# A chunked scan beside a projection stream: products inside chunks in longer runs, decays prepared on ScalarE, loads and gate units re-ordered

## The chip, the cores and the metric

The kernel runs on one core of a Trainium2 chip. The metric is device time in microseconds, the median of several executions of the whole program; lower is better. TensorE multiplies matrices, VectorE and ScalarE work on elements, GpSimd does little here, and SyncE (SP) issues the DMA transfers, one after another.

## The reference, cut to what matters

One layer of a hybrid backbone on 1152 tokens (1024 latent tokens in eight chunks of 128, and 128 context tokens, chunk 8). The change lies in the Mamba-2 scan, which runs in two directions for 32 heads of 64 channels:

```python
a_cs = cumsum(a within the chunk)                   # a = dt * A
L = exp(where(mask, a_cs[i] - a_cs[j], -inf))
CB = einsum("bcign,bcjgn->bcgij", Cc, Bc)
y_diag = einsum("bcgrij,bcjgrp->bcigrp", CB[:, :, :, None] * L, x)      # inside chunks
states = einsum("bcjgn,bcgrj,bcjgrp->bcgrpn", Bc, exp(a_cs[..., -1:] - a_cs), x)
h_final, h_prev = scan(h -> exp(a_cs[..., -1]) * h + states)            # from chunk to chunk
y_off = einsum("bcign,bcgri,bcgrpn->bcigrp", Cc, exp(a_cs), h_prev)     # from earlier chunks
y = y_diag + y_off          # then both directions are added, + D * x, times silu(z)
```

Here x carries a factor dt. Around the scan stand an input projection of 1024 by 9280 columns (z, x, B, C, dt, u, v and two branch gates ga, gb), a gated MLP branch, the merge, the output projection and a ConvFFN. All is float32.

## The kernel before

**Stages.** The projection is done in blocks of 128 output channels. One block takes 3 token blocks of 384 and 24 matmuls for each (8 contraction blocks, and a high and a low part of each factor: hi*hi, lo*hi, hi*lo). Its matmuls write the PSUM tile `gps` (lines 301 to 303, three banks). Weights come in tiles of 128x512 (`wr`); ScalarE makes the high part (`wh`, line 84) and VectorE the low part (`wl`, line 85). `conv_gen` (x, B, C), `z_unit` and `gate_unit` use the result; a gate unit only copies it out (line 610) and stores it.

**The scan beside it.** The scan works on 16 pairs of heads, q = 0 to 15, four to a group of B and C. `rounds[q]` lists the projection blocks that run while pair q is scanned: x of the next pair, z of the pair before, at the end of a group also B and C of the next, and `NGATE[q]` gate units. `merge` spreads the scan's steps evenly over the round's block slots (3 to a block). Steps are raised in priority by `P_SCAN` = 50. Each engine's instructions are put in order when the program is built, by priority and planned time, and run on the chip in that order.

**A pair's steps.** With s = 0 to 3 for two chunks each and s = 4 for the context chunk:

- `ssd_loads(q, s)`: SP loads `R` (the cumulative sums of both directions and heads, spread over the partitions, three buffers), `EP` (the same for the factor of `y_off`, two buffers), and with s = 4 the start state `H`.
- `mstage(s)`: makes exp(a_cs - a_cs' + ln dt) from R. The shift by `nb` goes to ScalarE for the first four of up to eight pieces (`NACT`, line 672) and to VectorE for the rest (line 674, with a clamp at 60). VectorE clamps the first four (line 677), ScalarE takes the exponentials of R (line 678) and EP (line 680), VectorE multiplies by `CB` (line 688) and adds the directions (line 689).
- `chain(s)`: the states. VectorE scales Xtok into `xwf`, `xwb` (line 694), TensorE multiplies by B into the one bank `pst` (lines 709, 710), VectorE carries `H` along (lines 713, 715).
- `ctx_state()`: the context's final state through the same bank (line 724), copied out (line 725).
- `main(s)`: TensorE makes `yo` (from the states, line 740) and `yd` (inside chunks, line 744: for each chunk one matmul per head, each on 64 of the 128 columns of the array, `tile_position=(0, 64 * h)`). VectorE joins them with X (lines 749 to 754).

The order of a pair's steps:

```python
pro = [step((mstage, 4), (chain, 0)), step((mstage, 0), (chain, 1)), step((chain, 2)), step((chain, 3))]
outs = [step((mstage, 1), (main, 4), (ssd_loads, q, 2)), step((mstage, 2), (main, 0), (ssd_loads, q, 3), (ctx_state,)),
        step((mstage, 3), (main, 1), (nxt, 4)), step((main, 2), (nxt, 0)), step((main, 3), (nxt, 1))]
```

A round holds the five `outs` of its pair and, unless a new group begins, the four `pro` of the next; the first round of a group also its own `pro`: 13, 9, 9 and 5 steps. In the trace a float32 matmul of the scan is two records, so a `main` of two chunks leaves eight records of line 744.

**Ahead of the scan.** `decays` turns dt into `nb` = ln dt - a_cs (line 513), `wst`, `cdk`, and stores the cumulative sums for the loads.

**Behind it.** The scan's memory is given to the gated MLP's tiles, among them `wsT`, which the matmul of line 849 reads.

Of the kernel before, what the change touches and what calls it, by code (L numbers as in the profile page):

```python
# [4 lines left out]
F32 = mybir.dt.float32  # L5
F32R = mybir.dt.float32r
AF = mybir.ActivationFunctionType
# [7 lines left out]
NL = 1024  # L15
# [15 lines left out]
MT_DT, MT_U, MT_B, MT_C, MT_X, MT_Z, MT_GA, MT_GB = 0, 1, 9, 13, 17, 33, 49, 57  # L31


NGATE = [1, 1, 1, 0, 1, 1, 1, 0, 1, 1, 1, 0, 1, 1, 1, 0, 0]

NACT = 4

NXM, NWM, GBUF = 4, 10, 7

# [1 line left out]

LASTK = 4

P_SCAN, P_HT, P_MOD, P_DECAY = 50, 100, 200, 200


def gcol(t):
    return t if t < NL else t + 1
# [60 lines left out]
def body(tc, A, O):  # L109
# [202 lines left out]
    def tbank(name):  # L312
        return pt_.tile([128, 512], F32, tag="t", name=name)
# [134 lines left out]
    k_cm, kp = pool("tok")  # L448
    nb = kp.tile([128, NC, 64], F32, name="nb")
    wst = kp.tile([128, NC, 64], F32, name="wst")  # L450
    cdk = kp.tile([128, 8, 2, 32], F32, name="cdk")
    sb_cm, spb = pool("ssdB")
    u_cm, up = pool("dt")
# [29 lines left out]
    def decays():  # L483
        for src, dst in ((xd, dtt), (xa, adt)):
            ps = tbank("pdt")
            for i in range(4):
                PE.transpose(ps[:, 128 * i:128 * i + 128], src[:, 128 * i:128 * i + 128], ident)
            pv = ps.rearrange("p (c m) -> p c m", m=128)
            S.copy(dst[:, 0:4, :], pv[:, :, 0:64])
            V.tensor_copy(dst[:, 5:9, :], pv[:, :, 64:128])  # L490
        ps = tbank("pdt4")
        for j, src in enumerate((xd, xa)):
            PE.transpose(ps[:, 128 * j:128 * j + 128], src[:, 512:640], ident)
        for j, dst in enumerate((dtt, adt)):
            V.tensor_copy(dst[:, 4, :], ps[:, 128 * j:128 * j + 64])
        for d in range(2):
            a_d = adt[:, :, 32 * d:32 * d + 32]
            for lhs, dst in (((Lo, Up)[d], acst), (ones, tot)):
                pv = tbank(f"pacs{d}")[:, :288].rearrange("p (c h) -> p c h", h=32)
                PE.matmul(pv, lhsT=lhs, rhs=a_d, start=True, stop=True)  # L500
                V.tensor_copy(dst[:, :, 32 * d:32 * d + 32], pv)
        rows = up.tile([64, NC, 128], F32, name="rows")
        for b in range(3):
            ps = tbank(f"prow{b}")
            for i in range(3):
                PE.transpose(ps[:64, 128 * i:128 * i + 128], acst[:, 3 * b + i, :], ident)
            V.tensor_copy(rows[:, 3 * b:3 * b + 3, :], ps[:64, :384].rearrange("p (c m) -> p c m", m=128))
        for d in range(2):
            for h in range(2):
                SP.dma_start(acs_scr[:, d, h], rows[32 * d + h:32 * d + 32:2, :, :])  # L510
        V.tensor_scalar(lndt, dtt, 1e-18, None, op0=ALU.max)
        S.activation(lndt, lndt, AF.Ln)
        V.tensor_tensor(nb, lndt, acst, op=ALU.subtract)
        V.tensor_tensor(wst, tot, acst, op=ALU.subtract)
        S.activation(wst, wst, AF.Exp)
        V.tensor_tensor(wst, wst, dtt, op=ALU.mult)
        S.activation(cdk[:, :, 0, :], tot[:, 0:8, 0:32], AF.Exp)
        for k in range(8):
            S.activation(cdk[:, k, 1, :], tot[:, 7 - k, 32:64], AF.Exp)
# [107 lines left out]
    def cc_of(s):  # L627
        return [2 * s, 2 * s + 1] if s < 4 else [8]

    Rt, EPt, Ht = {}, {}, {}  # L630

    def ssd_loads(q, s):

        cc = cc_of(s)
        n = len(cc)
        R = spa.p.tile([128, 2, 2, 2, 128], F32, tag="R", name=f"R{q}{s}", bufs=3)
        if n == 2:
            SP.dma_start(R.rearrange("p d h c i -> p (d h) (c i)"),
                         acs_scr[q, :, :, cc[0]:cc[0] + 2].rearrange("d h c i -> (d h) (c i)").unsqueeze(0).to_broadcast([128, 4, 256]))
        else:  # L640
            SP.dma_start(R[:, :, :, 0, :].rearrange("p d h i -> p (d h) i"),
                         acs_scr[q, :, :, cc[0]].rearrange("d h i -> (d h) i").unsqueeze(0).to_broadcast([128, 4, 128]))
        Rt[q, s] = R
        if s < 4:
            E = spa.p.tile([128, 2, 2, 128], F32, tag="EP", name=f"EP{q}{s}", bufs=2)
            for h in range(2):
                SP.dma_start(E[64 * h:64 * h + 64].rearrange("p d c i -> p d (c i)"),
                             acs_scr[q, :, h, cc[0]:cc[0] + 2].rearrange("d c i -> d (c i)").unsqueeze(0).to_broadcast([64, 2, 256]))
            EPt[q, s] = E
        if s == 4:  # L650
            H = spa.p.tile([128, 8, 2, 128], F32, tag="H", name=f"H{q}", bufs=2)
            SP.dma_start(H[:, 0], A["h0"][q])
            Ht[q] = H

    def ssd(q):

# [1 line left out]
        _, Bt, CT, CB = groups[g]  # L658
        X, Xt = xq[q]
        Dc = par[:, P_D + q:P_D + q + 1]  # L660

        def mstage(s):
            cc = cc_of(s)
            n = len(cc)
            R = Rt[q, s]
            for d in range(2):
                for h in range(2):
                    col = 32 * d + 2 * q + h
                    for i, c in enumerate(cc):
                        r = R[:, d, h, i, :]  # L670
                        if 4 * d + 2 * h + i < NACT:
                            S.activation(r, r, AF.Identity, bias=nb[:, c, col:col + 1])  # L672
                        else:
                            V.tensor_scalar(r, r, nb[:, c, col:col + 1], 60.0, op0=ALU.add, op1=ALU.min)
            Rv = R.rearrange("p d h c i -> p (d h) c i")[:, :, :n]
            if NACT:
                V.tensor_scalar(Rv[:, :NACT // 2], Rv[:, :NACT // 2], 60.0, None, op0=ALU.min)
            S.activation(Rv, Rv, AF.Exp)
            if s < 4:
                S.activation(EPt[q, s], EPt[q, s], AF.Exp)  # L680
            for d in range(2):
                if n == 2:
                    r = R[:, d].rearrange("p h c i -> p h (c i)")
# [2 lines left out]
                    r = R[:, d, :, 0, :]  # L686
                    cb = CB[:, d, cc[0], :].unsqueeze(1).to_broadcast([128, 2, 128])
                V.tensor_tensor(r, r, cb, op=ALU.mult)
            V.tensor_tensor(R[:, 0, :, :n], R[:, 0, :, :n], R[:, 1, :, :n], op=ALU.add)

        def xw(c0, n, d, dst):

# [24 lines left out]
        def ctx_state():  # L717
# [7 lines left out]
            S.copy(so, ps[:, 0])  # L725
            for d in range(2):
                SP.dma_start(O[2 + d][0, 0, 2 * q:2 * q + 2].rearrange("h p n -> (h p) n"), so[:, d, :])

        def main(s):
            cc = cc_of(s)  # L730
            n = len(cc)
            R = Rt.pop((q, s))
            o = gcol(128 * cc[0])
            if s < 4:
                H = Ht[q]
                yo = pyo.tile([128, 2, 2, 128], F32, tag="yo", name=f"yo{q}{s}")
                for i, c in enumerate(cc):
                    for d in range(2):
                        k = c if d == 0 else 7 - c
                        PE.matmul(yo[:, d, i, :], lhsT=H[:, k, d, :], rhs=CT[:, 128 * c:128 * c + 128], start=True, stop=True)  # L740
            yd = pyd.tile([128, 512], F32, tag="yd", name=f"yd{q}{s}")[:, :128 * n]
            for i, c in enumerate(cc):
                for h in range(2):
                    PE.matmul(yd[64 * h:64 * h + 64, 128 * i:128 * i + 128], lhsT=Xt[:, c, 64 * h:64 * h + 64],  # L744
                              rhs=R[:, 0, h, i, :], start=True, stop=True, tile_position=(0, 64 * h))
            xv = X[:, o:o + 128 * n]
            if s < 4:
                E = EPt.pop((q, s))
                V.tensor_tensor(E, E, yo, op=ALU.mult)
                V.scalar_tensor_tensor(xv, xv, Dc, E[:, 0].rearrange("p c i -> p (c i)"), op0=ALU.mult, op1=ALU.add)  # L750
                V.tensor_tensor(xv, xv, E[:, 1].rearrange("p c i -> p (c i)"), op=ALU.add)
                V.tensor_tensor(xv, xv, yd, op=ALU.add)
            else:
                V.scalar_tensor_tensor(xv, xv, Dc, yd, op0=ALU.mult, op1=ALU.add)

        def nxt(s):
            if q + 1 < 16:
                ssd_loads(q + 1, s)

        def step(*fs):  # L760
            def run():
                for f, *a in fs:
                    f(*a)
            return run
        pro = [step((mstage, 4), (chain, 0)), step((mstage, 0), (chain, 1)), step((chain, 2)), step((chain, 3))]
        outs = [step((mstage, 1), (main, 4), (ssd_loads, q, 2)), step((mstage, 2), (main, 0), (ssd_loads, q, 3), (ctx_state,)),
                step((mstage, 3), (main, 1), (nxt, 4)), step((main, 2), (nxt, 0)), step((main, 3), (nxt, 1))]
        return pro, outs

    def merge(fills, steps):  # L770
# [35 lines left out]
    gtp.p, gtp.bufs = spa.p, 1  # L806
    run_unit(first_x)
    for s in (4, 0, 1):
        ssd_loads(0, s)
    after = None  # L810
    for q in range(17):
        steps = []
# [538 lines left out]
```

## Time and profile before

| | us |
|---|---|
| median of 3 runs (2471.34 to 2474.54) | 2472.48 |
| the profiled execution | 2474.21 |
| its span, first to last instruction | 2472.1 |
| TensorE (PE) busy | 2428.6 |
| VectorE (DVE) busy | 1853.4 |
| ScalarE (ACT) busy | 1110.5 |

PE is matmuls and PEld weight loads, which overlap them. A row of the timeline gives start, length, engine, line, operation, tiles (out<-in), shapes and how many records of a kind follow each other; matmuls are pipelined, so a record's length is more than the time to the next one's start. A group's row gives the busy time and the mean of one, and behind the second bar the engine's idle time before it and what ended it. In square brackets stands the idle time before a single row.

### The profile page before, as it was taken

The numbers are of one execution on the slowest core, as the hardware profiler recorded it, in microseconds if no ns is written. First come the engines' busy times: TensorE is split into PE (matmuls) and PEld (weight loads), VectorE is DVE, ScalarE is ACT, GpSimd is POOL, SyncE is SP. The second block draws the span as 40 slices with busy tenths as digits, with TensorE's granted clock in tenths as the row PEclk, the third lists the DMA queues.
The fourth block names the chain that finished last, engine by engine and source line by source line (L and its number), as shares of the span: only waits on it lengthen the run. The fifth ranks groups of instructions, "written<-read, shape, count | busy, mean of one in ns | idle before, by whom it ended". The sixth has DMA issues, their size and how long they took to land.

```text
span 2472.1 us, 37398 instructions
## 1 busy us (share of the span) xinstructions
PE 2428.6 (98%) x13951; PEld 2271.1 (92%) x13951; DVE 1853.4 (75%) x3150; ACT 1110.5 (45%) x2118; POOL 28.4 (1%) x82
## 2 busy tenths in 40 slices
PE   7989999999999999999999999999999999999998
PEld 5989999999999998899999998999999999998777
DVE  5668988878878884983546657459999989998554
ACT  5545655555555553211445545354333433344443
POOL 0000000000000000000000000000000000000000
PEclk9999999999999999999999999999999999999999
DMA  6134334433433444641456657442212221114674
GB/s 257 39 96 146 123 125 141 136 95 117 140 101 103 149 123 157 214 150 62 148 163 206 210 161 237 153 139 76 71 65 71 69 68 61 66 64 135 217 244 132
DMA packets 204182, 323.21 MB, mean 131 GB/s; under 512 B 19329, under 2 KB 113313, under 8 KB 203873
## 3 DMA queue, kind: packets, MB, share of 16 engines
q1 hardware_dynamic: 204000, 320.82, 40.5%
q8 instruction: 110, 1.80, 0.3%
q14 instruction: 72, 0.58, 0.1%
HBM read 278.22 MB, written 42.52 MB: 130 GB/s over the span
## 4 chain that ended last, share of the span: by engine, by line
PE 89%; DMA 6%; DVE 2%; ACT 1%; issue 1%; SPq 0%; POOL 0%; DVEq 0%; POOLq 0%; ACTq 0%
PE gps L301 10%; PE gps L303 10%; PE gps L302 10%; PE pup L302 7%; PE pup L303 7%; PE pup L301 7%; PE fo L1167 4%; PE fo L1169 4%; PE fo L1168 4%; PE yo L740 2%; PE yd L744 2%; PE pbs L301 2%; PE pbs L302 2%; PE pbs L303 2%; PE pv L865 1%; PE pv L866 1%
## 5 line engine op out<-in xcount | busy, mean ns | idle before, releaser
L85 DVE TENSOR_TENSOR wl<-wr,wh 128x512 fp32r<-128x512 f32 x544 | 371.7, 689 | 250.5 <-ACT wh L84 241.7
L84 ACT CAST wh<-wr 128x512 fp32r<-128x512 f32 x544 | 333.9, 619 | 471.3 <-PE pup L302 121.6
L301 PE MATMUL gps<-hh,wh 128*128 128x384 f32 x1512 | 518.2, 343 | 0.2 <-ACT pad L356 0.2
L303 PE MATMUL gps<-hh,wl 128*128 128x384 f32 x1512 | 513.9, 340 | 0.0
L302 PE MATMUL gps<-hl,wh 128*128 128x384 f32 x1512 | 513.4, 340 | 0.0
L1155 DVE SCALAR_TENSOR_TENSOR acc<-U,fpar,acc 128x960 f32<-128x960 f32 (+1 forms) x352 | 444.3, 1267 | 16.0 <-ACT acc L1148 8.2
L302 PE MATMUL pup<-h2l,wh 128*128 128x384 f32 x1056 | 353.1, 334 | 0.0
L301 PE MATMUL pup<-h2h,wh 128*128 128x384 f32 x1056 | 352.9, 334 | 0.0
L303 PE MATMUL pup<-h2h,wl 128*128 128x384 f32 x1056 | 352.4, 334 | 0.0
L301 PEld LDWEIGHTS gps<-hh,wh 128*128 128x128 f32 x1512 | 284.8, 188 | 6.4 <-issue 5.5
L302 PEld LDWEIGHTS gps<-hl,wh 128*128 128x128 f32 x1512 | 284.9, 188 | 3.9 <-issue 3.8
L303 PEld LDWEIGHTS gps<-hh,wl 128*128 128x128 f32 x1512 | 284.6, 188 | 4.1 <-issue 4.1
L301 PEld LDWEIGHTS pup<-h2h,wh 128*128 128x128 f32 x1056 | 198.2, 188 | 1.3
L302 PEld LDWEIGHTS pup<-h2l,wh 128*128 128x128 f32 x1056 | 198.2, 188 | 1.3
L303 PEld LDWEIGHTS pup<-h2h,wl 128*128 128x128 f32 x1056 | 198.2, 188 | 0.0
L1137 ACT COPY U<-pup 128x384 f32<-128x384 f32 (+1 forms) x132 | 58.4, 443 | 225.1 <-PE pup L303 225.1
L672 ACT ACTIVATE R<-R,nb 128x128 f32<-128x128 f32 x288 | 93.2, 391 | 136.6 <-DMA R<-acs_scr 132.5
L1167 PE MATMUL fo<-wh,gh 128*128 128x512 f32 x384 | 148.1, 397 | 0.3 <-ACT wh L84 0.3
L1168 PE MATMUL fo<-wh,gl 128*128 128x512 f32 x384 | 148.3, 396 | 0.0
L1169 PE MATMUL fo<-wl,gh 128*128 128x512 f32 x384 | 139.8, 396 | 0.0
L301 PE MATMUL pbs<-ysh,wh 128*128 128x384 f32 x384 | 129.8, 338 | 3.6 <-ACT wh L84 1.8
L303 PE MATMUL pbs<-ysh,wl 128*128 128x384 f32 x384 | 129.7, 338 | 0.2
(303 smaller groups left out, 3965.7 us busy)
## 6 DMA issues: line engine op xcount, KB each, us to landing
wr<-in_w_dn SPq DMA_DIRECT2D x132, 256.0 KB, 2.9
wr<-in_w_in SPq DMA_DIRECT2D x130, 256.0 KB, 2.9
R<-acs_scr SPq DMA_DIRECT2D x64, 512.0 KB, 4.1
wr<-in_w_bs SPq DMA_DIRECT2D x96, 256.0 KB, 3.4
wr<-in_w_up SPq DMA_DIRECT2D x90, 256.0 KB, 2.6
EP<-acs_scr SPq DMA_DIRECT2D x128, 128.0 KB, 3.2
wmt<-in_w_modt SPq DMA_DIRECT2D x32, 512.0 KB, 3.8
wr<-in_w_bu SPq DMA_DIRECT2D x48, 256.0 KB, 2.8
```

The costliest lines, as they stand in the source:

```text
L84: self.nc.scalar.copy(hi, w)
L85: self.nc.vector.tensor_tensor(lo, w, hi.bitcast(F32), op=ALU.subtract)
L301: PE.matmul(ps, lhsT=wh, rhs=xh, start=first and k == 0, stop=False)
L302: PE.matmul(ps, lhsT=wh, rhs=xl, start=False, stop=False)
L303: PE.matmul(ps, lhsT=wl, rhs=xh, start=False, stop=last and k == n - 1)
L672: S.activation(r, r, AF.Identity, bias=nb[:, c, col:col + 1])
L740: PE.matmul(yo[:, d, i, :], lhsT=H[:, k, d, :], rhs=CT[:, 128 * c:128 * c + 128], start=True, stop=True)
L1137: S.copy(u[:, a // 64:b // 64, 1:65], src.rearrange("p (r c) -> p r c", c=64))
L1155: tap = V.scalar_tensor_tensor(av[:, r0:r1], u[:, r0 + dy - 1:r1 + dy - 1, dx:dx + 64], w[i], av[:, r0:r1], op0=ALU.mult, op1=ALU.add)
L1167: PE.matmul(outs[c][h], lhsT=mh[:, cs_], rhs=wh, start=k == 0, stop=False)
L1168: PE.matmul(outs[c][h], lhsT=ml[:, cs_], rhs=wh, start=False, stop=False)
L1169: PE.matmul(outs[c][h], lhsT=mh[:, cs_], rhs=wl, start=False, stop=k == NFF - 1)
```

## The change

- **Runs.** The yd part of `main` becomes `within(b)`: four chunks at once for b = 0 (issued after main(1)), four and the context chunk for b = 1 (after main(3)). The summed R goes to a tile `RS` of four chunks; the context chunk's product goes to the unused half of `ctx_state`'s PSUM bank. The matmuls are raised by `P_RUN` = 400, and each is ordered behind the first of its run. `main` keeps yo.
- **Shift and clamp.** `nb` becomes a_cs - ln dt + top, where `top` is the largest ln dt of all. ScalarE takes relu(nb - R) for all pieces and exp(top - that); both clamps on VectorE go.
- **Order.** `chain` comes ahead of `mstage` in `pro`. Loads are split into `load_R`, `load_E`, `load_H`; E of s = 2, 3 is loaded a step later, and its exponential is taken in `main`.
- **Gate units.** `NGATE` is 2, 1, 0, 0 in each group where it was 1, 1, 1, 0.

```diff
-NGATE = [1, 1, 1, 0, 1, 1, 1, 0, 1, 1, 1, 0, 1, 1, 1, 0, 0]
-NACT = 4
+NGATE = [2, 1, 0, 0, 2, 1, 0, 0, 2, 1, 0, 0, 2, 1, 0, 0, 0]
-P_SCAN, P_HT, P_MOD, P_DECAY = 50, 100, 200, 200
+P_SCAN, P_HT, P_MOD, P_DECAY, P_RUN = 50, 100, 200, 200, 400
 # decays
-        V.tensor_tensor(nb, lndt, acst, op=ALU.subtract)
+        V.tensor_reduce(top, lndt.rearrange("p c m -> p (c m)"), axis=AX.X, op=ALU.max)
+        tops = up.tile([128, 128], F32, name="tops")
+        V.tensor_copy(tops, top.to_broadcast([128, 128]))
+        ps = tbank("ptop")
+        PE.transpose(ps[:, :128], tops, ident)
+        V.tensor_reduce(top, ps[:, :128], axis=AX.X, op=ALU.max)
+        V.tensor_tensor(nb, acst, lndt, op=ALU.subtract)
+        V.tensor_scalar(nb, nb, top, None, op0=ALU.add)
 # mstage
-                        if 4 * d + 2 * h + i < NACT:
-                            S.activation(r, r, AF.Identity, bias=nb[:, c, col:col + 1])
-                        else:
-                            V.tensor_scalar(r, r, nb[:, c, col:col + 1], 60.0, op0=ALU.add, op1=ALU.min)
+                        S.activation(r, r, AF.Relu, scale=-1.0, bias=nb[:, c, col:col + 1])
-            if NACT:
-                V.tensor_scalar(Rv[:, :NACT // 2], Rv[:, :NACT // 2], 60.0, None, op0=ALU.min)
-            S.activation(Rv, Rv, AF.Exp)
+            S.activation(Rv, Rv, AF.Exp, scale=-1.0, bias=top)
...
-            V.tensor_tensor(R[:, 0, :, :n], R[:, 0, :, :n], R[:, 1, :, :n], op=ALU.add)
+            V.tensor_tensor(sum_, R[:, 0, :, :n], R[:, 1, :, :n], op=ALU.add)
 # ctx_state
+            RS[3] = ps[:, 1, 0, :]
...
+        def within(b):
+            yd = pyd.tile([128, 512], F32, tag="yd", name=f"yd{q}{b}")
+            todo = [(yd[:, 128 * i:128 * i + 128], 4 * b + i, RS[b][:, :, i]) for i in (2, 3, 0, 1)]
+            if b == 1:
+                yc = RS[3]
+                todo.append((yc, 8, RS[2][:, :, 0]))
+            first = None
+            with tc.high_priority(offset=P_RUN):
+                for p, c, r in todo:
+                    for h in range(2):
+                        m = PE.matmul(p[64 * h:64 * h + 64], lhsT=Xt[:, c, 64 * h:64 * h + 64], rhs=r[:, h, :],
+                                      start=True, stop=True, tile_position=(0, 64 * h))
+                        if first is None:
+                            first = m
+                        else:
+                            queue_behind(m, first)
+            xv = X[:, 512 * b:512 * b + 512]
+            V.tensor_tensor(xv, xv, yd, op=ALU.add)
+            if b == 1:
+                xv = X[:, gcol(NL):gcol(NL) + 128]
+                V.scalar_tensor_tensor(xv, xv, Dc, yc, op0=ALU.mult, op1=ALU.add)
...
-        pro = [step((mstage, 4), (chain, 0)), step((mstage, 0), (chain, 1)), step((chain, 2)), step((chain, 3))]
+        pro = [step((chain, 0), (mstage, 4)), step((chain, 1), (mstage, 0)), step((chain, 2)), step((chain, 3))]
+        outs = [step((mstage, 1), (load_R, q, 2)), step((mstage, 2), (main, 0), (load_R, q, 3), (load_E, q, 2), (ctx_state,)),
+                step((mstage, 3), (main, 1), (within, 0), (load_E, q, 3), (nxt, load_R, 4), (nxt, load_H)),
+                step((main, 2), (nxt, load_R, 0), (nxt, load_E, 0)), step((main, 3), (within, 1), (nxt, load_R, 1), (nxt, load_E, 1))]
 # before round 0
-        ssd_loads(0, s)
+        load_R(0, s)
+        if s < 4:
+            load_E(0, s)
+    load_H(0)
```

More of the change, by code (lines that the diff above doesn't have):

```diff
@@ L450, in body @@
     wst = kp.tile([128, NC, 64], F32, name="wst")
+    top = kp.tile([128, 1], F32, name="top")
     cdk = kp.tile([128, 8, 2, 32], F32, name="cdk")
@@ L630, in body, with load_R @@
     Rt, EPt, Ht = {}, {}, {}
-    def ssd_loads(q, s):
+    def load_R(q, s):
         cc = cc_of(s)
-        n = len(cc)
         R = spa.p.tile([128, 2, 2, 2, 128], F32, tag="R", name=f"R{q}{s}", bufs=3)
-        if n == 2:
+        if len(cc) == 2:
             SP.dma_start(R.rearrange("p d h c i -> p (d h) (c i)"),
@@ L643, in ssd_loads, with load_E, load_H @@
         Rt[q, s] = R
[L644 to L653, printed above, removed]
+    def load_E(q, s):
+        cc = cc_of(s)
+        E = spa.p.tile([128, 2, 2, 128], F32, tag="EP", name=f"EP{q}{s}", bufs=2)
+        for h in range(2):
+            SP.dma_start(E[64 * h:64 * h + 64].rearrange("p d c i -> p d (c i)"),
+                         acs_scr[q, :, h, cc[0]:cc[0] + 2].rearrange("d c i -> d (c i)").unsqueeze(0).to_broadcast([64, 2, 256]))
+        EPt[q, s] = E
+    def load_H(q):
+        H = spa.p.tile([128, 8, 2, 128], F32, tag="H", name=f"H{q}", bufs=2)
+        SP.dma_start(H[:, 0], A["h0"][q])
+        Ht[q] = H
     def ssd(q):
@@ L660, in ssd @@
         Dc = par[:, P_D + q:P_D + q + 1]
+        RS = {}
         def mstage(s):
@@ L664, in mstage @@
             n = len(cc)
-            R = Rt[q, s]
+            R = Rt.pop((q, s))
+            if s == 4:
+                RS[2] = spa.p.tile([128, 2, 1, 128], F32, tag="RSc", name=f"RSc{q}", bufs=2)
+            elif s % 2 == 0:
+                RS[s // 2] = spa.p.tile([128, 2, 4, 128], F32, tag="RS", name=f"RS{q}{s}", bufs=2)
+            sum_ = RS[s // 2][:, :, 2 * (s % 2):2 * (s % 2) + n]
             for d in range(2):
@@ L670, in mstage @@
                         r = R[:, d, h, i, :]
-                        if 4 * d + 2 * h + i < NACT:
-                            S.activation(r, r, AF.Identity, bias=nb[:, c, col:col + 1])
-                        else:
-                            V.tensor_scalar(r, r, nb[:, c, col:col + 1], 60.0, op0=ALU.add, op1=ALU.min)
+                        S.activation(r, r, AF.Relu, scale=-1.0, bias=nb[:, c, col:col + 1])
             Rv = R.rearrange("p d h c i -> p (d h) c i")[:, :, :n]
-            if NACT:
-                V.tensor_scalar(Rv[:, :NACT // 2], Rv[:, :NACT // 2], 60.0, None, op0=ALU.min)
-            S.activation(Rv, Rv, AF.Exp)
+            S.activation(Rv, Rv, AF.Exp, scale=-1.0, bias=top)
             if s < 4:
-                S.activation(EPt[q, s], EPt[q, s], AF.Exp)
+                exp_E(s)
             for d in range(2):
@@ L688, in mstage, with exp_E @@
                 V.tensor_tensor(r, r, cb, op=ALU.mult)
-            V.tensor_tensor(R[:, 0, :, :n], R[:, 0, :, :n], R[:, 1, :, :n], op=ALU.add)
+            V.tensor_tensor(sum_, R[:, 0, :, :n], R[:, 1, :, :n], op=ALU.add)
+        def exp_E(s):
+            if s < 2:
+                S.activation(EPt[q, s], EPt[q, s], AF.Exp)
         def xw(c0, n, d, dst):
@@ L727, in ctx_state @@
                 SP.dma_start(O[2 + d][0, 0, 2 * q:2 * q + 2].rearrange("h p n -> (h p) n"), so[:, d, :])
+            RS[3] = ps[:, 1, 0, :]
         def main(s):
             cc = cc_of(s)
[L731 to L740, printed above, removed]
@@ L741, in main @@
-            yd = pyd.tile([128, 512], F32, tag="yd", name=f"yd{q}{s}")[:, :128 * n]
-            for i, c in enumerate(cc):
[L743 to L754, printed above, removed]
@@ L756, in nxt @@
-        def nxt(s):
+            o = 128 * cc[0]
+            H = Ht[q]
+            yo = pyo.tile([128, 2, 2, 128], F32, tag="yo", name=f"yo{q}{s}")
+            for i, c in enumerate(cc):
+                for d in range(2):
+                    k = c if d == 0 else 7 - c
+                    PE.matmul(yo[:, d, i, :], lhsT=H[:, k, d, :], rhs=CT[:, 128 * c:128 * c + 128], start=True, stop=True)
+            xv = X[:, o:o + 256]
+            E = EPt.pop((q, s))
+            if s >= 2:
+                S.activation(E, E, AF.Exp)
@@ new lines, in main @@
+            V.tensor_tensor(E, E, yo, op=ALU.mult)
+            V.scalar_tensor_tensor(xv, xv, Dc, E[:, 0].rearrange("p c i -> p (c i)"), op0=ALU.mult, op1=ALU.add)
+            V.tensor_tensor(xv, xv, E[:, 1].rearrange("p c i -> p (c i)"), op=ALU.add)
+        def within(b):
[7 more added lines that the diff above has]
+                for p, c, r in todo:
+                    for h in range(2):
+                        m = PE.matmul(p[64 * h:64 * h + 64], lhsT=Xt[:, c, 64 * h:64 * h + 64], rhs=r[:, h, :],
[9 more added lines that the diff above has]
+                V.scalar_tensor_tensor(xv, xv, Dc, yc, op0=ALU.mult, op1=ALU.add)
@@ L757, in nxt @@
+        def nxt(f, *a):
             if q + 1 < 16:
-                ssd_loads(q + 1, s)
+                f(q + 1, *a)
         def step(*fs):
@@ L764, in step @@
             return run
-        pro = [step((mstage, 4), (chain, 0)), step((mstage, 0), (chain, 1)), step((chain, 2)), step((chain, 3))]
-        outs = [step((mstage, 1), (main, 4), (ssd_loads, q, 2)), step((mstage, 2), (main, 0), (ssd_loads, q, 3), (ctx_state,)),
-                step((mstage, 3), (main, 1), (nxt, 4)), step((main, 2), (nxt, 0)), step((main, 3), (nxt, 1))]
+        pro = [step((chain, 0), (mstage, 4)), step((chain, 1), (mstage, 0)), step((chain, 2)), step((chain, 3))]
+        outs = [step((mstage, 1), (load_R, q, 2)), step((mstage, 2), (main, 0), (load_R, q, 3), (load_E, q, 2), (ctx_state,)),
+                step((mstage, 3), (main, 1), (within, 0), (load_E, q, 3), (nxt, load_R, 4), (nxt, load_H)),
+                step((main, 2), (nxt, load_R, 0), (nxt, load_E, 0)), step((main, 3), (within, 1), (nxt, load_R, 1), (nxt, load_E, 1))]
         return pro, outs
```

## The prediction

> **What bounds the kernel now.** I read the page's shares and chain first, then the busy time by stretches, then TensorE's waits, and last the order of TensorE's instructions inside the scan.
>
> ```profile
> span 2472.1 us, 37398 instructions
> PE 2428.6 (98%) x13951; PEld 2271.1 (92%) x13951; DVE 1853.4 (75%) x3150; ACT 1110.5 (45%) x2118; POOL 28.4 (1%) x82
> PE 89%; DMA 6%; DVE 2%; ACT 1%; issue 1%; SPq 0%; POOL 0%; DVEq 0%; POOLq 0%; ACTq 0%
> ```
> ```profile
> 60.00:145.00 85.00, 77.95 (x448) 74.18 (x446) 56.27 (x91) 44.34 (x85) 0.30 (x3) 0.96 0.21 62
> 145.00:950.00 805.00, 804.20 (x5210) 761.84 (x5210) 663.49 (x1480) 437.94 (x848) 3.96 (x36) 1.00 0.39 121
> 950.00:1216.00 266.00, 262.15 (x1410) 242.20 (x1409) 163.31 (x300) 56.74 (x100) 4.54 (x3) 0.99 0.47 153
> ```
> ```profile
> PE ptX L549 <- ACT Xtok L550: 5.7, 2, 4.9
> PE prs L849 <- DMA wsT<-in_sgu_w: 3.2, 1, 3.2
> PE pst L709 <- DVE xwf L694: 0.2, 1, 0.2
> ```
>
> The columns of the second fence are the stretch, its length, then busy time of PE, PEld, DVE, ACT, POOL, then granted clock and DMA. The scan is the stretch 145 to 950: TensorE is busy for 804.2 of 805 us, VectorE for 663, ScalarE for 438. So time is won there only by taking work from TensorE's queue; VectorE and ScalarE matter where they make it wait, and the third fence says they hardly do: the large wait, 4.9 us, lies ahead of the scan, the next, 3.2 us, behind it.
>
> But busy is not free of loss. The rows below show TensorE around the products inside chunks (yd, line 744).
>
> ```profile
> 947.45 0.33 PE L301 MATMUL gps<-hh,wh 128*128 128x384 f32 x1
> 947.62 0.34 PE L302 MATMUL gps<-hl,wh 128*128 128x384 f32 x1
> 947.89 0.66 PE L744 MATMUL yd<-R,Xtok 128*64 128x128 f32 x8
> 948.48 0.44 PE L303 MATMUL gps<-hh,wl 128*128 128x384 f32 x1
> 948.76 0.34 PE L301 MATMUL gps<-hh,wh 128*128 128x384 f32 x1
> ```
> ```profile
> 249.37 0.34 PE L301 MATMUL gps<-hh,wh 128*128 128x384 f32 x1
> 249.64 0.44 PE L744 MATMUL yd<-R,Xtok 128*64 128x128 f32 x4
> 250.01 0.45 PE L302 MATMUL gps<-hl,wh 128*128 128x384 f32 x1
> 250.29 0.34 PE L303 MATMUL gps<-hh,wl 128*128 128x384 f32 x1
> ```
> ```profile
> 526.15 0.42 PE L302 MATMUL gps<-hl,wh 128*128 128x384 f32 x1
> 526.50 0.43 PE L744 MATMUL yd<-R,Xtok 128*64 128x128 f32 x2
> 526.86 0.44 PE L303 MATMUL gps<-hh,wl 128*128 128x384 f32 x1
> ...
> 528.70 0.43 PE L744 MATMUL yd<-R,Xtok 128*64 128x128 f32 x2
> 529.06 0.45 PE L303 MATMUL gps<-hh,wl 128*128 128x384 f32 x1
> 529.34 0.34 PE L301 MATMUL gps<-hh,wh 128*128 128x384 f32 x1
> ```
>
> Undisturbed, gps matmuls start 0.17 us apart (947.45, 947.62). With eight yd records between, the second gps behind starts 948.76 - 947.62 = 1.14 us after the last one ahead: 1.14 - 2 x 0.17 = 0.80 us for two chunks. With four records: 250.29 - 249.37 - 0.34 = 0.58 us for one chunk. So a visit to yd costs 0.36 us fixed (2 x 0.58 - 0.80) and 0.22 us a chunk. The fixed part sits at its ends: 0.27 us ahead of it and 0.28 us behind its first successor, where 0.17 is normal. In the third fence one main is torn into four visits of two records (one head each): 529.34 - 526.15 = 3.19 us less five spacings (0.85) is 2.34 us, 0.58 us each, where the same work in one visit takes 0.80.
>
> **Part 1: runs of four.** How many visits are there?
>
> ```profile
> L744 PE MATMUL yd<-R,Xtok x576: 272/273/324, 150.7 to 948.3; 128*64 128x128 f32 x192
> 150.68 0.44 PE L744 MATMUL yd<-R,Xtok 128*64 128x128 f32 x4
> ```
>
> The 576 records form, in order of start, 109 stretches without another line between: 53 of eight, 3 of six, 14 of four, 39 of two; the first is this row at 150.68, the last that at 947.89. Cost now: 56 x 0.80 + 14 x 0.58 + 39 x 0.58 = 75.5 us. After: `within(0)` issues four chunks and `within(1)` five, raised by P_RUN and ordered behind their first matmul, so 32 visits: 16 x (0.36 + 0.88) + 16 x (0.36 + 1.10) = 43.2 us. Gain 32.3 us. If visits are torn as often as now, only the merging counts, 3 fewer visits for each of 16 q: 48 x 0.36 = 17.3 us. I take 32.3: each run's first matmul waits for the newest sum (chunks 2 and 3), so the others have nothing left to wait for, and 400 against 50 puts them ahead of the gps stream that tears them now. On VectorE, 64 adds of yd become 32 of double width; it is not the bound.
>
> **Part 2: shift and clamp on ScalarE.**
>
> ```profile
> L672 ACT ACTIVATE R<-R,nb 128x128 f32<-128x128 f32 x278 | 89.9, 391 | 128.1 <-DMA R<-acs_scr 124.0 <-PE gps L303 2.3 <-PE yd L744 1.7
> L674 DVE TENSOR_SCALAR R<-R,nb 128x128 f32<-128x128 f32 x278 | 62.8, 281 | 46.4 <-DMA R<-acs_scr 45.9
> L677 DVE TENSOR_SCALAR R<-R 128x512 f32<-128x512 f32 (+1 forms) x78 | 30.8, 395 | 3.8 <-ACT R L672 3.4
> ```
> ```profile
> 139.56 0.88 DVE L674 TENSOR_SCALAR R<-R,nb 128x128 f32<-128x128 f32 x4 [2.94 <-DMA R<-acs_scr]
> 139.56 1.28 ACT L672 ACTIVATE R<-R,nb 128x128 f32<-128x128 f32 x4 [2.28 <-DMA R<-acs_scr]
> ...
> 144.37 1.06 ACT L678 ACTIVATE R<-R 128x1024 f32<-128x1024 f32 x1
> ```
>
> 288 shifts (16 q x 18; 278 of them inside the scan's stretch) move from line 674 to ScalarE and the 80 clamps of line 677 go. Four in a row take 1.28 us on ScalarE, 0.32 each: +92 us, 438 to 530 in a scan of some 773, 69%. VectorE loses 63 + 31 us and falls to about 570, 74%. Neither is full, so the cost for TensorE is nothing while the slack holds; the rivals price it gone. The Trainium skill, ScalarE: Activation LUTs, rules for kernel authors, sends relu, min and add to VectorE and not to ScalarE. The rows agree on the unit price (0.32 against 0.22 us), and by that rule the move loses 0.10 x 288 = 29 us of engine time; the sum ignores it, since TensorE waits for neither. Relu is not in this trace. If it forced ScalarE to change tables around each of 72 stages, two loads each would cost 72 x 2 x 1.28 = 185 us of ScalarE; at the other end nothing.
>
> ```profile
> L512 ACT ACT_TABLE_LOAD x1 | 1.3, 1283 | 0.0
> ```
>
> I take nothing: identity, exp, tanh and square alternate through the whole scan and it holds no table load. The same page, section on table sets, says relu stands in every set.
>
> The bound `top` adds to the decays a maximum over 576 columns, a broadcast copy, one transpose and its maximum, and a second pass over nb.
>
> ```profile
> 124.60 0.75 DVE L513 TENSOR_TENSOR nb<-lndt,acst 128x576 f32<-128x576 f32 x1
> ```
>
> At this row's 0.75 us or less for each of two wide passes, and less for the narrow ones, that is up to 2.5 us of VectorE in a stretch where TensorE already idles 7 us; hidden it is 0. I take +1.
>
> **Part 3: chain first, loads split.** The 4.9 us wait ahead of the scan is a transpose of X waiting for the Xtok copy, which stands on ScalarE behind R's shifts (139.56, after 2.28 us for R's landing). With eight shifts and the exponential no longer waiting for a clamp, that copy could come 1.28 + 1.06 us later; with the H load behind the R loads and chain, which needs Xtok, first, it could come before them. Bounds -4.9 and +2.4; I take -1, the middle. The SP queue carries the same loads; E of steps 2 and 3 no longer stands with its R, and R's buffer is free after the sum and not after the matmul, so SP blocks less; I count nothing, because TensorE waits for no load in the scan. `yc` now sits in the one pst bank from ctx_state to the end of within(1), so chain(0) of the next q queues behind a VectorE add. The present wait of that matmul is 0.2 us in all; bounds 0 and 15 x 1 us, I take +1.
>
> **Part 4: gate units.** Twelve before, twelve after, 72 gps matmuls each (12.4 us). Rounds 0, 4, 8, 12 gain one, rounds 2, 6, 10, 14 lose one: there 9 steps stand beside 6 block slots, 24.8 us of gps. In round 14 the loss thins what covers the scan's end.
>
> ```profile
> 965.56 2.50 PE L849 MATMUL prs<-wsT,cst 128*128 128x512 f32 x4 [3.20 <-DMA wsT<-in_sgu_w]
> ```
>
> This wait hangs on the scan's memory coming free, after the last yd at 947.89. A later scan end lengthens it: 0 to 12.4 us, I take +2, near the present wait. For new waits inside the scan, 0 to 34 (rival 2), I take +1.
>
> **Sum.** The profiled execution took 2474.2 us (span 2472.1), 1.7 above the median of 2472.5. 2474.2 - 32.3 + 1 - 1 + 1 + 2 + 1 = 2445.9; against the median 2444.
>
> **Rivals.**
> 1. *Half the gain* (chance 0.2): visits are still torn, or starts and tail take the rest: 2472.5 - 17.3, and the other terms' +4: 2459. For it: 39 of 109 visits are torn now. Against: the new order and priority.
> 2. *ScalarE decides the thin rounds* (chance 0.14: 0.04 still faster, 0.05 the same, 0.05 slower).
>
> ```profile
> ACT EP L680 <- DMA EP<-acs_scr: 52.4, 40, 3.9
> ```
>
> Per q ScalarE has 530 / 16 = 33 us of work and (124 + 52) / 16 = 11 us of waiting for R and EP, which hold up all behind them, weight casts and evacuations of gps: 44 us. A thin round gives TensorE 24.8 + about 11 us of scan matmuls. Not absorbed by the next round (12 slots, 49.5 us), that is 8.5 x 4 = 34 us: 2444 + 34 = 2478, slower, and more if landings take longer. From two thirds not absorbed on (23 of 34 us) the gain is gone to within 0.2%; slower needs nearly all of it. Against it: in the whole scan 16 x 44 = 706 us stays under 773, and R's earlier release shortens the waits.
> 3. *The visit's fixed price isn't saved* (0.05): if it belonged to each chunk, the visits of eight would cost 1.16 and not 0.80; then 2472.
>
> **How the numbers follow.** Forecast 0.61, rivals 0.2, 0.14, 0.05. A measurement can tell 0.2%, 5 us: faster means under 2467.5. Faster 0.61 + 0.2 + 0.04 = 0.85; same 0.05 + 0.05 = 0.10; slower 0.05. The range runs from 2433 (the wait ahead of the scan gone too, and no new waits) to 2465 (rival 1 with a thinner tail). The forecast's own range is 2433 to 2453.
>
> **What would show it.** Line 744's successor in 32 visits of 16 and 20 records, some 1.25 and 1.45 us each; TensorE's scan stretch near 773 us and still full; ScalarE near 530, VectorE near 570; no table load. Wrong if visits of two remain, if gps waits for wh or for a bank behind relu, or if prs waits over 10 us.

## The result, and the profile after

The changed kernel takes 2454.97 us (median of 4 runs, 2451.83 to 2456.71) against 2473.51 us of the kernel before in the same sessions: ratio 0.9922, 95% interval 0.9905 to 0.9939, 18.5 us faster. The forecast was 2444 with a range of 2433 to 2465; the direction held, and two thirds of the forecast gain arrived. The profiled execution took 2456.7 us, 17.5 less than that of before.

The page of the changed kernel, with its span, its shares and its chain:

```profile
span 2454.9 us, 37306 instructions
PE 2401.7 (98%) x13952; PEld 2270.2 (92%) x13952; DVE 1782.0 (73%) x2754; ACT 1193.9 (49%) x2406; POOL 27.7 (1%) x82
PE 85%; DMA 6%; DVE 4%; ACT 4%; issue 1%; SPq 1%; POOL 0%; DVEq 0%; ACTq 0%; POOLq 0%
```

The stretches of the scan up to the first v matmul, which starts at 940.06 and started at 956.04 before (columns as in the prediction), first in the kernel before, then in the changed one, here with the stretch behind it:

```profile
145.00:956.00 811.00, 810.20 (x5244) 767.84 (x5244) 666.42 (x1483) 442.04 (x854) 3.96 (x36) 1.00 0.39 121
```
```profile
145.00:940.00 795.00, 781.44 (x5244) 765.47 (x5244) 594.83 (x1092) 522.52 (x1133) 3.54 (x36) 0.99 0.40 123
940.00:1200.00 260.00, 256.90 (x1362) 236.27 (x1363) 160.79 (x297) 52.15 (x94) 4.53 (x3) 0.98 0.47 155
```

TensorE has 28.8 us less to do in the scan (781.4 us, was 810.2), but it is no longer full: it is idle for 13.6 us, where it was idle for 0.8. So the scan is 16 us shorter where 32 less, and TensorE still full, were forecast. VectorE fell from 666 to 595, ScalarE rose from 442 to 523. TensorE's waits say where it stands now:

```profile
PE pv L900 <- ACT vwh L82: 7.6, 1, 7.6
PE yo L755 <- DMA H<-in_h: 4.8, 1, 4.8
PE yd L775 <- DVE X L782: 3.1, 4, 1.3
PE prs L884 <- DMA wsT<-in_sgu_w: 2.8, 1, 2.8
...
PE yo L755 <- DVE H L731: 0.9, 1, 0.9
PE pst L725 <- DVE H L731: 0.7, 2, 0.5
```

The first row is new at this length; in the kernel before that wait was:

```profile
PE pv L865 <- ACT vwh L84: 0.4, 1, 0.4
```

The second row stands where the transposes of X waited 4.9 us. The third row and the last two lie inside the scan, which had almost no waits (0.8 us). TensorE's order around the products, a visit of 16 records and one of 20 (16 into yd, 4 into the context bank):

```profile
387.33 0.34 PE L301 MATMUL gps<-hh,wl 128*128 128x384 f32 x1
387.60 1.09 PE L775 MATMUL yd<-RS,Xtok 128*64 128x128 f32 x16
388.62 0.44 PE L299 MATMUL gps<-hh,wh 128*128 128x384 f32 x1
388.90 0.33 PE L300 MATMUL gps<-hl,wh 128*128 128x384 f32 x1
```
```profile
422.70 0.34 PE L300 MATMUL gps<-hl,wh 128*128 128x384 f32 x1
422.97 1.09 PE L775 MATMUL yd<-RS,Xtok 128*64 128x128 f32 x16
423.89 0.39 PE L775 MATMUL pstc<-RSc,Xtok 128*64 128x128 f32 x4
424.21 0.45 PE L301 MATMUL gps<-hh,wl 128*128 128x384 f32 x1
424.49 0.34 PE L299 MATMUL gps<-hh,wh 128*128 128x384 f32 x1
```

Less two spacings of 0.17 us these are 388.90 - 387.33 - 0.34 = 1.23 us and 424.49 - 422.70 - 0.34 = 1.45 us; 1.24 and 1.46 were forecast. All 32 visits are whole: 16 of each kind, 42.9 us at these two prices where 75.5 were. The Trainium skill, TensorEngine Tiling (Array Packing), key properties, says that a change of the tiling mode drains TensorE; the trace fits it, with a fixed price of 0.36 us a visit.

### The profile page after: what moved, and what is told of

Its sections match the earlier page's. It is cut to its first block, busy times and chain, and to the rows that moved or that the text cites. A ratio compares the mean times of both kernels' runs of the same rounds, so it can differ in the third digit from the quotient of the medians.

```text
span 2454.9 us, 37306 instructions
## 1 busy us (share of the span) xinstructions
PE 2401.7 (98%) x13952; PEld 2270.2 (92%) x13952; DVE 1782.0 (73%) x2754; ACT 1193.9 (49%) x2406; POOL 27.7 (1%) x82
## 4 chain that ended last, share of the span: by engine, by line
PE 85%; DMA 6%; DVE 4%; ACT 4%; issue 1%; SPq 1%; POOL 0%; DVEq 0%; ACTq 0%; POOLq 0%
PE gps L299 9%; PE gps L300 9%; PE gps L301 9%; PE pup L300 7%; PE pup L299 7%; PE pup L301 7%; PE fo L1202 4%; PE fo L1204 4%; PE fo L1203 4%; PE pbs L299 2%; PE pbs L301 2%; PE pbs L300 2%; PE yo L755 2%; DMA R<-acs_scr 1%; PE pv L900 1%
## 5 line engine op out<-in xcount | busy, mean ns | idle before, releaser
L688 ACT ACTIVATE R<-R,nb 128x128 f32<-128x128 f32 x576 | 179.6, 392 | 47.2 <-DMA R<-acs_scr 46.8
```

The source lines that it names most:

```text
L688: S.activation(r, r, AF.Relu, scale=-1.0, bias=nb[:, c, col:col + 1])
```

## The experiments

Ratios are to the kernel before on the same chip, with 95% intervals.

### The runs alone

```diff
 # the kernel before, with RS, within(0), within(1) and P_RUN of the change
-step((mstage, 1), (main, 4), (ssd_loads, q, 2))
+step((mstage, 1), (ssd_loads, q, 2))
-step((mstage, 3), (main, 1), (nxt, 4))
+step((mstage, 3), (main, 1), (within, 0), (nxt, 4))
-step((main, 3), (nxt, 1))
+step((main, 3), (within, 1), (nxt, 1))
```

> The kernel before with the longer runs alone (the tile RS, within(0) and within(1), P_RUN); shift, clamp, order of chain, loads and gate units as before. Theory A (the gain is the visits to the products' array mode, 109 to 32, 32 us of TensorE): TensorE's rows of yd in 32 visits of 16 and 20 records, 1.23 and 1.44 us each, and with the old gate units still covering the scan's end the time is 2442 to 2450. Rival B (VectorE must be relieved of shift and clamp before TensorE can use the gain): VectorE over 90% in the scan, new waits of TensorE on VectorE's sums of over 10 us in all, time 2455 to 2466.

Measured: 2521.65 us, ratio 1.0191 (1.0177 to 1.0206), 47 us slower. The visits were whole, 16 and 16. Both theories miss the time. B names the right engine, but VectorE is not full (636.5 of the 805 us from 145 to 950), and TensorE waits for H and not for the sums. TensorE's longest waits:

```profile
PE pst L715 <- DVE H L721: 38.9, 5, 10.8
```

The pst matmul is chain's. All five waits stand in the third pair of a group (they end at 276.5 and 287.6, 504.7, 727.0 and 933.5); why there, no run shows. Here is the first, VectorE ahead (its own queue in order), then TensorE:

```profile
268.46 0.41 DVE L721 TENSOR_TENSOR H<-H,pst 128x256 f32<-128x256 f32 x1
...
270.26 0.41 DVE L683 TENSOR_SCALAR R<-R 128x512 f32<-128x512 f32 x1
270.60 0.86 DVE L680 TENSOR_SCALAR R<-R,nb 128x128 f32<-128x128 f32 x4
271.38 0.41 DVE L719 TENSOR_TENSOR H<-H,cdk 128x256 f32<-128x256 f32 x1
...
272.65 0.41 DVE L683 TENSOR_SCALAR R<-R 128x512 f32<-128x512 f32 x1
272.99 0.86 DVE L680 TENSOR_SCALAR R<-R,nb 128x128 f32<-128x128 f32 x4
273.77 0.41 DVE L683 TENSOR_SCALAR R<-R 128x512 f32<-128x512 f32 x1
...
275.98 0.41 DVE L721 TENSOR_TENSOR H<-H,pst 128x256 f32<-128x256 f32 x1
```
```profile
276.53 0.77 PE L715 MATMUL pst<-xwf,Btok 128*128 128x128 f32 x2 [6.50 <-DVE H L721]
```

chain(0)'s second add of H (275.98) frees the one pst bank for chain(1). Between chain's instructions on VectorE stand shifts (line 680) and clamps (683), 3 us of the 7.5 from 268.46, beside other work. TensorE stands in front of its matmul with gps behind it. The 38.9 us are not the whole loss. The other waits in the scan add up to 17.8 us, the first v tile waits 8.0 longer than before, and the clock of TensorE stood at half for more of its work (46.5 us, was 15.4; at half the pace an estimated 15.5 us lost, see the last section). With the 32.6 us that the visits save this gives some +48; the profiled executions differ by 46.6.

### Which of the two: the held bank or VectorE's queue

```diff
 # the runs alone, and
-                todo.append((yc, 8, RS[2][:, :, 0]))      # context product in ctx_state's bank
+        def main4():                                      # by itself in the yd bank, in outs[0]
```

> The kernel before with the longer runs, but the context chunk's product by itself in the yd bank as before, so that the one pst bank is free as soon as ctx_state's copy is made. The runs alone gave 2521 us, with 39 us of TensorE waiting before chain's first matmul (pst) for VectorE's H. Theory E (the shifts and clamps that wait on VectorE for R's landings stand ahead of H in its queue): these waits stay, 25 us or more, time 2505 to 2530. Rival F (the context product holds the pst bank until the end of within(1)): they fall under 8 us, time 2455 to 2485.

Measured: 2463.64 us, 0.9958 (0.9942 to 0.9974). Rival F: 38.9 us of waits became 3.5, and the kernel is 58 us faster than with the runs alone, although each pair pays one visit more.

```profile
PE pst L715 <- DVE H L721: 3.5, 6, 1.3
PE pst L715 <- ACT so L731: 3.5, 3, 2.4
```

With `yc` in the pst bank, chain(0) of the next pair begins only behind its read in within(1), and then its H work falls among the next shifts. The traces show the order, here for the third pair, first with the runs alone (the read, then chain(0)), then with the bank free (chain(0), then within(1) of the second pair):

```profile
262.02 0.34 DVE L774 SCALAR_TENSOR_TENSOR X<-X,par,pstc 128x128 f32<-128x128 f32 x1
265.30 0.38 PE L715 MATMUL pst<-xwf,Btok 128*128 128x128 f32 x2
```
```profile
241.97 0.38 PE L715 MATMUL pst<-xwf,Btok 128*128 128x128 f32 x2
252.24 1.09 PE L760 MATMUL yd<-RS,Xtok 128*64 128x128 f32 x16
```

With the runs alone chain(0) stands behind the context product in all 15 pairs that follow another, by 3.7 to 6.2 us.

### Runs, with shift and clamp on ScalarE

```diff
 # the runs alone (context product in the pst bank), and
-  ScalarE and VectorE shift, VectorE clamps at 60
+  S.activation(r, r, AF.Relu, scale=-1.0, bias=nb[...]), exp with scale=-1.0, bias=top
```

> The kernel before with the longer runs and with shift and clamp on ScalarE; order of chain, loads and gate units as before, the context product in ctx_state's bank. The runs alone gave 2521 us. Theory K (the held bank hurts only while H stands behind VectorE's shifts and clamps; without these VectorE frees it in time): waits of pst on VectorE under 3 us, 2440 to 2453. Rival: the held bank costs TensorE 20 us or more whatever VectorE does, and it was the order of chain and the loads that mended it in the changed kernel, 2470 to 2500.

Measured: 2448.09 us, 0.9898 (0.9882 to 0.9914). Theory K: the wait of pst on H, 38.9 us, is 0.6.

```profile
PE pv L888 <- ACT vwh L84: 6.5, 2, 5.9
...
PE prs L872 <- DMA wsT<-in_sgu_w: 1.6, 1, 1.6
PE pst L718 <- DVE H L724: 0.6, 3, 0.2
```

So there are two cures for the same wait: free the bank, or take the shifts out of VectorE's queue. The change held the bank and took the second. These two parts alone reach the whole gain of the change; their median is 7 us lower, but the intervals overlap.

### The change without its shift and clamp

```diff
-S.activation(r, r, AF.Relu, scale=-1.0, bias=nb[:, c, col:col + 1])
+four pieces S.activation(Identity), four V.tensor_scalar(add, min 60); clamp of the first four on VectorE; no top
```

> The changed kernel with shift and clamp as before (four pieces on ScalarE, four on VectorE, both clamps on VectorE at 60, nb as before, no top). Theory A (shift and clamp lie beside TensorE's work): 2450 to 2460, as the changed kernel; VectorE's busy time in the scan about 90 us higher, ScalarE's about 90 lower, TensorE's scan stretch the same to within 5 us. Rival B: 2462 or more, with waits of TensorE behind VectorE.

Measured: 2498.62 us, 1.0097 (1.0084 to 1.0111): 44 us above the changed kernel. Rival B. Neither engine is full (up to the first v matmul VectorE is busy for 669 of 841 us, ScalarE for 440), yet TensorE waits for VectorE: 19.7 us in front of chain, and its waits in the scan are 37 us in all, where the changed kernel has 5.

```profile
PE pst L722 <- DVE H L728: 19.7, 5, 8.3
```

### The change without its runs

```diff
-(within, 0), (within, 1)
+products(s) in main(s), two chunks at a time into yd; chunk 8 by itself in outs[0]
```

> The changed kernel with the products again two chunks at a time, in main, and the context chunk by itself; all else as changed. Theory A: about 80 visits or more come back and the kernel keeps only what the other parts cost (the 8 us wait ahead of the first v tile, some 6 us of small waits): 2475 to 2488, at or above the kernel before. Rival B: at least a third of the gain stays, 2455 to 2467.

Measured: 2487.39 us, 1.0053 (1.004 to 1.0066), 32 us above the changed kernel; theory A. The trace has 127 visits again (49 of eight, 65 of two). TensorE is full and simply has more to do:

```profile
145.00:963.00 818.00, 817.69 (x5236) 768.73 (x5236) 588.78 (x1118) 516.75 (x1125) 3.54 (x36) 1.00 0.38 118
```

### Runs without their priority

```diff
-            with tc.high_priority(offset=P_RUN):
...
-                        else:
-                            queue_behind(m, first)
```

> The changed kernel with within's matmuls at the scan's own priority and without the order behind the first. Theory A: runs are torn as they were before; from 48 stretches (16 of them the context state's own) to 100 or more, each torn piece 0.36 us more, 2470 to 2485. Rival: gathering them in one step is enough, the stretches stay under 60 and the time 2450 to 2460.

Measured: 2482.58 us, 1.0032 (1.0022 to 1.0043). Theory A: 103 visits in place of 32 (58 of them of two records), and 71 x 0.36 = 25.6 us is most of the 27.6 us lost against the changed kernel. Gathering the products in one step is worth little by itself (2482.58 against 2487.39 without the runs); the priority and the order keep them together. Which of these two does it was not tried.

### Gate units in their old rounds, and one behind the scan

```diff
-NGATE = [2, 1, 0, 0] * 4 + [0]
+NGATE = [1, 1, 1, 0] * 4 + [0]                          # first kernel
+NGATE = [2, 1, 0, 0] * 3 + [1, 1, 0, 0] + [1]           # second kernel
```

> The changed kernel with the gate units in their old rounds (1, 1, 1, 0 in each group). Theory C (round 14 lost the block that covered the scan's end, so TensorE runs out of work 8 us before the memory of the scan is free): the wait of the first v tile on its weight's cast falls from 7.6 us to under 2, time 2444 to 2451. Rival D (rounds of thirteen steps need the extra block): the wait goes, but the first rounds of the groups stand 10 us or more on VectorE and ScalarE, time 2453 to 2465.

> The changed kernel with one gate unit moved from round 12 to round 16, behind z of the last pair (2, 1, 0, 0 three times, then 1, 1, 0, 0, 1). Theory C2 (TensorE runs out of blocks at the scan's end): 12.4 us of gps cover the last steps, the 7.6 us wait of the first v tile goes, 2446 to 2450. Rival I (the scan's steps have their own pace there, and end as much later as work is moved behind them): the wait stays over 5 us, or waits of the same length appear in rounds 12 to 15, 2452 to 2458.

Measured: 2449.76 us, 0.9897 (0.9882 to 0.9912), and 2451.44 us, 0.9909 (0.9893 to 0.9925). Theories C and C2 fall: the wait of the first v tile stayed at 7.8 us in both, although the time with the old rounds lies in theory C's range.

```profile
PE pv L900 <- ACT vwh L82: 7.8, 1, 7.8
```
```profile
PE pv L900 <- ACT vwh L82: 7.8, 1, 7.8
```

Rival D falls too: with the old rounds the scan holds one wait of 2.3 us, of a transpose of X that ends at 274.7, and none of 10. With the old rounds the waits of yd inside the scan (3.1 us) are gone and the median is 5 us lower, but the intervals meet at the edge; that the new rounds cost something is likely, not shown.

### E loaded early again, alone and with the old gate rounds

```diff
-step((mstage, 1), (load_R, q, 2)), ... (load_R, q, 3), (load_E, q, 2) ... (within, 0), (load_E, q, 3)
+step((mstage, 1), (load_R, q, 2), (load_E, q, 2)), ... (load_R, q, 3), (load_E, q, 3) ... (within, 0)
-            if s >= 2:  S.activation(E, E, AF.Exp)       # in main; now in mstage for all s
```

> The changed kernel with E of steps 2 and 3 loaded a step earlier again, beside its R, and its exponential in mstage as before. Theory J (the late load and exponential of E hold up the last two mains, so TensorE runs out of blocks before the scan's last step): the 7.6 us wait of the first v tile falls under 3 us, time 2444 to 2450. Rival I (the scan's pace at the end has another cause): the wait stays at 7 to 8 us, time 2452 to 2458.

> The same, and the gate units in their old rounds as well. By theory J and the 5 us that the old rounds gave alone (2450): 2439 to 2446. By rival I: 2448 to 2453, with the wait of 7 to 8 us as in the kernel with the old rounds alone.

Measured: 2453.38 us, 0.9919 (0.9904 to 0.9933), and 2451.32 us, 0.9905 (0.9889 to 0.9922). Theory J falls: the wait of the first v tile is 7.6 and 7.8 us.

### H loaded early

```diff
-    R(4), R(0), E(0), R(1), E(1), then load_H(0)
+    R(4), load_H(0), then R(0), E(0), R(1), E(1)
```

> The changed kernel with the first pair's H loaded right behind R of the context chunk, as before, not behind all its R and EP. Theory G (TensorE's 4.8 us wait ahead of the scan is on that load): the wait goes; 2450 to 2453. Rival H (the Xtok copy behind ScalarE's shifts is next, the 4.9 us of the kernel before): the wait only changes its name, 2453 to 2457.

Measured: 2455.52 us, 0.9924 (0.9909 to 0.9938). Rival H: the 4.8 us on H are gone, and the transposes wait for Xtok's copies behind ScalarE's shifts.

```profile
PE ptX L556 <- ACT Xtok L557: 6.5, 2, 3.3
```

### What makes the wait at the scan's end

In the changed kernel, ScalarE and TensorE at the scan's end:

```profile
936.02 1.06 ACT L605 ACTIVATE z<-X 128x1024 f32<-128x1024 f32 x1 [5.19 <-DVE X L604]
937.11 1.26 ACT L607 ACTIVATE X<-X,par 128x1153 f32<-128x1153 f32 x1
938.27 1.22 ACT L617 COPY gt<-gps 128x384 f32<-128x384 f32 x3
939.37 1.68 ACT L82 CAST vwh<-wr 128x512 fp32r<-128x512 f32 x3
```
```profile
931.19 1.05 PE L755 MATMUL yo<-CT,H 128*128 128x128 f32 x8
940.06 0.80 PE L900 MATMUL pv<-vwh,hh 128*128 128x512 f32 x1 [7.64 <-ACT vwh L82]
```

The last yo starts at 931.19; one gps matmul is left behind it. What follows it on VectorE and ScalarE takes until 939.4, and only then come the casts of v's weights. In the kernel before, 54 gps matmuls were left. The gate units and E did not move this, so I freed the bank:

```diff
 # runs with shift and clamp on ScalarE, and
-            RS[3] = ps[:, 1, 0, :]
-                yc = RS[3]
+                yc = tbank(f"yc{q}")[:, :128]
```

> The kernel before with the longer runs and with shift and clamp on ScalarE, as in runs_relu (2448 us), and the context chunk's product in one of the two banks of the transposes (tbank), taken in within(1), in place of ctx_state's pst bank; no visit is added. Theory F2 (the held pst bank lets chain of the next pair begin only behind within(1), the pairs go one after another, the scan lags and TensorE runs out of blocks 6 to 8 us before its end): the wait of the first v tile falls under 2 us, 2438 to 2444. Rival I (the scan's pace at the end has another cause): the wait stays over 5 us, 2445 to 2451; if the transposes now wait for their bank, their waits of over 3 us in all show it.

Measured: 2448.31 us, 0.9900 (0.9883 to 0.9917). Theory F2 has its mechanism: 47 gps matmuls are left behind the last yo where the same kernel with the held bank had 11, and the wait is 1.7 us in all and not 6.5.

```profile
924.09 1.05 PE L748 MATMUL yo<-CT,H 128*128 128x128 f32 x8
934.39 0.50 PE L887 MATMUL pv<-vwh,hh 128*128 128x512 f32 x1 [1.09 <-ACT vwh L84]
```
```profile
PE ptX L557 <- ACT Xtok L558: 3.6, 1, 3.6
...
PE pv L887 <- ACT vwh L84: 1.7, 2, 1.1
```

But the time did not follow: 2448 as without it, in the rival's range. Part of what was won stands in a longer wait ahead of the scan (3.6 us, was 2.2) and of prs (2.6, was 1.6), and three of the runs are torn (35 visits, 3 x 0.36 = 1.1 us); the rest is within the spread of the runs. One thing stays open: in the change without its runs the bank was free too, and the wait was 7.0 us. There TensorE had some 40 us more of visits, and why its scan ended behind the last block wasn't tried. The held bank is one cause of that lag, not the only one.

## Why the prediction was right or wrong

**Part 1 (runs)** held in its mechanism and its size: 32 visits, 42.9 us against 43.2, a gain of 32.6 against 32.3, and without the runs the changed kernel loses 32 us. The reason given for whole visits held as well: without priority and order there are 103.

**Part 2 (shift and clamp)** was right for the two kernels compared and wrong in its reason. The step that failed is "Neither is full, so the cost for TensorE is nothing while the slack holds", read from busy shares. The move is no neutral part: with the bank held, it is worth 44 us beside the other parts and 74 us (2521.65 - 2448.09) on the kernel with the runs alone. What counts is what stands ahead of chain's H in VectorE's queue. With the bank free the move is worth less: from the kernel with the context product by itself to that with `yc` in a bank of the transposes the time falls by 15.3 us (2463.64 to 2448.31), of which 15 visits fewer (50 and 35) are 5.4 at 0.36, so an estimated 10 us. ScalarE rose to 523 us in the scan, as forecast (530), holds no table load there, and its waits for R fell from 124.0 to 41.3 us (those for EP rose from 52.4 to 94.5):

```profile
L688 ACT ACTIVATE R<-R,nb 128x128 f32<-128x128 f32 x556 | 173.3, 392 | 41.8 <-DMA R<-acs_scr 41.3 <-DVE H L729 0.3
```

Rival 2, priced from the old waits, stayed away: inside the scan no gps matmul waits for a weight cast or for a bank. The bound for table loads counts 72 stages where there are 80 (16 x 5), so it would be 205 us and not 185; none was needed. The rule for kernel authors in the Trainium skill, ScalarE: Activation LUTs, gives relu to VectorE. The unit prices agree (eight relu in a row take 2.44 us on ScalarE, 0.31 each, against 0.22 for a shift on VectorE), but the kernel is 44 us faster with relu on ScalarE; the measurement decides. The bound `top`, +1 in the sum, shows no cost: ahead of the scan, from 60 to 145 us, TensorE is busy for 77.97 us, was 77.95.

**Part 3.** For `yc` in the pst bank the bounds 0 to 15 us were too narrow for what can happen: 38.9 us of waits in the kernel with the runs alone, 0.7 in the changed kernel (forecast +1). That the +1 came out is owed to part 2, which the prediction counted as neutral; it did not see this link, so the hit is luck. Its other cost, the lag of the scan's end, the prediction put on the gate units. Ahead of the scan the sum had -1; a 4.8 us wait on H, now the last load, took the place of 4.9 on Xtok, with 1.0 of that left over: +1. Chain first was not tried by itself; nothing in the runs shows that it bought anything.

**Part 4** took +2 for the scan's end, in the wait of prs. That wait fell, from 3.2 to 2.8 us; the cost came in the wait of the first v tile, which the prediction did not price: 7.6 us against 0.4 before, +7. This is the term of the sum that was mis-sized. The cause given, round 14's missing block, was wrong: the old rounds leave the wait at 7.8.

The sum, measured: -32.6 for the visits, +7 at the scan's end, +1 ahead of it, about +4 of waits inside it (yd 3.1, yo 0.9, pst 0.5 more; forecast +1 and +1) is -20.6; the profiled executions differ by -17.5. The 3 us between have the size of a cost that the sum lacked: around its longer waits TensorE works at half clock, for 23.1 us in the changed kernel and 15.4 before, an estimated 3.8 us lost (below).

## What to carry to other kernels

An engine that is not full can still hold up the one that is: read what stands ahead of the awaited instruction in its queue, not its busy share. A bank or buffer kept longer to save a step moves that queue's order; try the saving with the bank free and with the bank held before pricing it. Small matmuls in another array mode are priced by the visit, and a priority that keeps them together is part of the change.

## What the runs showed of the hardware

Longer waits of TensorE cost more than their length. The changed kernel's granted clock around the scan's end, two stretches (columns as above, the clock is the third number from the end):

```profile
936.20:943.00 6.80, 2.94 (x7) 2.36 (x8) 3.25 (x4) 4.82 (x8) 0.00 (x0) 0.50 0.55 153
949.80:956.60 6.80, 5.99 (x10) 3.43 (x11) 3.30 (x10) 1.86 (x3) 0.00 (x0) 0.50 0.86 338
```

Both begin inside a wait, of the first v tile (932.4 to 940.06) and of prs (947.9 to 950.61), and outlast it by 2.9 and 6.0 us; v matmuls start 0.43 us apart there (941.08, 941.51) and 0.23 us once the clock is back (944.04, 944.27). Over the whole run the clock stood at half for 22.7 us before, 36.0 after, 89.4 with the runs alone, in pieces that are multiples of 3.4 us except at the run's end. The Trainium skill, TensorE: Matmul & The Clock Gate, Part 1, gives a window of 3.4 us and half rate after an idle one. The trace agrees with the length and with the half rate; it does not show a whole idle window each time, since the second stretch begins 1.9 us into its wait.
